# Hybrid decoder layer: token rows, row factors and transposes in the first stage, 128-wide diagonal products and row ends

## The chip, the cores and the metric

The kernel runs on one core of one Trainium2 chip (trn2). The metric is device microseconds of one execution. Three timed runs of the kernel before took 1751.09, 1756.36 and 1757.32 us (median 1756.36). A separate profiled execution, from which all rows below are taken, took 1752.65 us.

## The reference

The layer has 2048 tokens and a model width of 1024, in float32. A condition vector `c` gives a shift, a scale and a gate per feature. The normalised tokens are modulated, projected to 4096 columns, used by two kinds of attention, gated and projected back:

```python
mod = (c @ w_ada + b_ada).astype(jnp.float32)
shift, scale, gate = jnp.split(mod, 3, axis=-1)
h = (_rmsnorm(x, norm_g) * (1.0 + scale[:, None, :]) + shift[:, None, :])
proj = h @ w_in       # sb_q, sb_k, sb_v, sb_g (512 each), df_q, df_k, df_v, df_g (512 each)
sb_out = _stick_breaking(...) * silu(sb_g)      # 8 heads of 64, strictly causal
df_out = _rmsnorm(_diff_attention(...), subln_g) * 0.8 * silu(df_g)   # 4 heads, two 64-wide maps each
out = concatenate([sb_out, df_out]) @ w_out
x = x + gate * out
```

`_rmsnorm` divides each token's row by the root of the mean of its squares over the 1024 features. The stick-breaking weight is `sigmoid(z_ts) * prod(1 - sigmoid(z_tj))` over the keys between s and t; the differential head is the difference of two softmaxes.

## The kernel before, in words

Every product of float32 matrices is split into a high and a low half (`hH`/`hL` of the activations, `wh`/`wl` of the weights, in the float32r type), and is the sum of three products (`mm3`, L318 to L320). The program is written as one long list of steps; a scheduler then sets the order on each engine by the dependences and its own estimate of times. Work with a later due time (`P`, the projections) is woven between the steps of the attention (`A`) by a planner with fixed costs (L1055 to L1166).

The first stage is what happens before the attention can start. It works on the first 1024 tokens in two chunks of 512:

- The chunk's `x` is loaded turned, feature rows by tokens, as eight tiles `xt` of 128x512 from `xT` (L68, L239). ScalarE squares them (L206, L209), VectorE adds the squares up (`xacc`, L210), TensorE turns the sums (`ps_c`, L198), and VectorE reduces them (L199) to a sum per token and makes the factor `rs_y` by eleven small instructions after L216 (L132 to L141: three steps of Newton's method). TensorE spreads the factor over the partitions (`ps_y`, L223), ScalarE copies it to `rb` (L226), and VectorE or GpSimd multiplies the eight tiles with it (L915, L918; L977 in the second chunk).
- Beside it the shift and the scale are made: `ada_block` (L163, L165) takes a 128x1024 tile `wada` of `w_ada`, multiplies it with `c` spread over the partitions (`cb`, loaded by a DMA at L899 into one of the six large buffers of tag `big`) and sums each row. There are two tiles for each 128 features (k), 16 in all, of 512 KB each; `gmul` (L947) is (1 + scale) times the norm's gain.
- `make_h` (L245 to L251) then makes `hH` and `hL` of one k: ScalarE's Identity with scale and bias, a cast, and a subtraction on VectorE or GpSimd.
- For each k, TensorE adds twelve 512-wide products to four PSUM tiles (`ps_p` for q, `ps_k` for k); these are followed by the v products of the chunk (`ps_n`, four blocks of 24 products, 256 wide), and by the same for the second chunk (q at 512 wide, then k, then v).
- Weights arrive as `raw` or `kraw` tiles (L299) and are split by a cast and a subtraction (L302/L304 and L306).
- Twenty transposes of the identity (L907) stand on TensorE ahead of the first sums.

All loads are issued by SyncE's queue, in order; each waits for its destination to be free and for an earlier DMA of its slot.

In the attention, a query block of 128 rows takes its scores against the keys in segments of 512 (`scores`, L482; the mask of the diagonal is one more 128-wide product, L485). Where the last segment is 128 keys long, it is computed 256 wide (`segs`). The weights of a pair of query blocks are turned (`ps_t`, L518), split into `aH` and `aL` (L524, L525) and multiplied with v (`av`, L598/L599 and L671 to L673), 256 queries wide. In the last group of keys of a pair the first 128 columns are zeros, written by two memsets on GpSimd (L522, L523).

Of the kernel before, what the change touches and what calls it, by code (L numbers as in the profile page):

```python
# [45 lines left out]
def build(ctx: ExitStack, tc, xT, cT, normg, w_adaT, b_ada, w_in, qg, kg, lam4, subg, w_out,  # L46
# [42 lines left out]
    def more_constants():  # L89
        nc.sync.dma_start(qgt, qg)  # L90
        nc.sync.dma_start(kgt, kg)
        nc.sync.dma_start(sgt, subg)
        tmp0 = ppool.tile([128, 512], F32, name="tmp0", tag="stg", bufs=NSTG)
        lamt = tmp0[:, 0:256].rearrange("p (f d) -> p f d", d=64)
        nc.sync.dma_start(lamt, lam4.unsqueeze(0).broadcast_to([128, 4, 64]))
        for h in range(NDF):
# [14 lines left out]
        nc.sync.dma_start(dist, distd)  # L111
# [131 lines left out]
    def make_h(k, ch, xt, hH, hL, act, pool=False):  # L243
        th, tl = hH[(k, ch)], hL[(k, ch)] = h_tiles(k, ch)
        nc.scalar.activation(xt, xt, AF.Identity, scale=gmul[:, k:k + 1], bias=mod[:, k:k + 1])  # L245
        if act:
            nc.scalar.copy(th, xt)
        else:
            nc.gpsimd.tensor_scalar(out=th, in0=xt, scalar1=1.0, scalar2=0.0, op0=ALU.mult,
                                    op1=ALU.add)  # L250
        (nc.gpsimd if pool else nc.vector).tensor_tensor(out=tl, in0=xt, in1=th.bitcast(F32),  # L251
                                                         op=ALU.subtract)
# [236 lines left out]
    def segs(n, ext):  # L489
        return [(o, min(512, n - o), min(512, ext - o, max(256, n - o))) for o in range(0, n, 512)]  # L490
# [10 lines left out]
    def back_steps(pair, A, get_av, acol, vmm):  # L501
# [3 lines left out]
        def up(st, g):  # L505
# [15 lines left out]
            if last:  # L521
# [376 lines left out]
    cb = big("cb")[:, 0:D]  # L898
    nc.sync.dma_start(cb, cT.unsqueeze(0).broadcast_to([128, D]))  # L899
    acc = stage("xacc")  # L900
    for k in range(KT):
        sq_add(acc, k, xa[0][k], nc.vector)

    def warm(n):
        wp = aps_.tile([128, 512], F32, name="av", tag="av")
        for j in range(n):
            nc.tensor.transpose(wp[:, 0:128], ident, ident)  # L907

    y0 = row_rstd(acc, nc.vector)
    warm(WARM[0])  # L910
    rb = spread(y0)
    warm(WARM[1])
    rs0 = rs_last[0]
    for k in range(3):
        nc.vector.tensor_tensor(out=xa[0][k], in0=xa[0][k], in1=rb, op=ALU.mult)  # L915
    w_q = load_w(w_in, C_SBQ, False)
    for k in range(3, KT):
        nc.gpsimd.tensor_tensor(out=xa[0][k], in0=xa[0][k], in1=rb, op=ALU.mult)  # L918
    w_k, kwl = [], None
    wa = {}  # L920
    for j in range(KT):
# [12 lines left out]
    def load_v():
        for kk in range(4):
            vwh = apool.tile([128, 2, 256], F32R, name="vwh", tag="kc", bufs=8)
            vwl = apool.tile([128, 2, 256], F32R, name="vwl", tag="kc", bufs=8)
            w_v.extend(load_w_part(w_in, C_SBV, kk, vwh, vwl))

    def load_x1():  # L940
        for k in range(KT):
            xa[1][k] = load_x(0, 1, k, apool.tile([128, 512], F32, name="xt", tag="vc", bufs=8))
    pq = [pps.tile([128, 512], F32, name="ps_p", tag="pj") for _ in range(2)]
    pk = [zps.tile([128, 512], F32, name="ps_k", tag="z") for _ in range(2)]
    for k in range(KT):
# [3 lines left out]
        ada_block(0, k, wa[(0, k)], cb)  # L949
        make_h(k, 0, xa[0][k], *hs[0], True, k in (2, 4, 6))  # L950
# [7 lines left out]
    after(ld, load_x1)  # L958
    acc = stage("xacc")
    for k in range(KT):  # L960
        sq_add(acc, k, xa[1][k], nc.vector)
# [207 lines left out]
_INS = ["xT", "cT", "normg", "w_adaT", "b_ada", "w_in", "qg", "kg", "lam4", "subg", "w_out",  # L1169
# [45 lines left out]
```

## Time and profile before

| | |
|---|---|
| timed runs (median of 3) | 1756.36 us |
| profiled execution | 1752.65 us |
| its span in the trace | 1750.9 us |
| TensorE busy | 1657.7 us (95%), 10740 matmuls |
| VectorE, ScalarE, GpSimd busy | 1258.4, 990.3, 890.0 us (72%, 57%, 51%) |
| first product of q and k starts | 42.44 us |
| first chunk's q and k done | about 72.6 us |
| second chunk's first product starts | 93.10 us |
| second chunk's q done, its k starts | 105.31 us |

Busy time of TensorE is counted from start to modelled end of each matmul, and consecutive matmuls overlap; what one costs in a dense stream is the distance between two starts. The granted clock is 1.00 where TensorE runs at 2.4 GHz, and 0.50 at 1.2 GHz.

### The profile page before, as it was taken

To read this page: it belongs to the slowest core of one execution; us is meant where nothing else is said; L and a number is where in the kernel's file an instruction comes from. 1 tells how busy PE (TensorE), PEld (TensorE's weight loads), DVE (VectorE), ACT (ScalarE), POOL (GpSimd) and SP (SyncE) were. 2 spreads that over 40 slices of the span, in tenths; PEclk is the share of its full clock that TensorE was granted. 3 is DMA by queue.
4 is the path that set the end of the run, shared out by engine and by line. 5 is a ranking of instruction groups with operands and counts; after the bars stand their busy time and mean duration, and the time that the engine had idled before them with its cause. 6 is when DMAs were issued, how large, how long until landed. Compare 5 with 4: busy or idle time off the path is not lost.

```text
span 1750.9 us, 31674 instructions
## 1 busy us (share of the span) xinstructions
PE 1657.7 (95%) x10740; PEld 1486.7 (85%) x10740; DVE 1258.4 (72%) x2558; ACT 990.3 (57%) x1997; POOL 890.0 (51%) x1454
## 2 busy tenths in 40 slices
PE   1889989999999999999999999999999999999999
PEld 1677879789999989878898888799998988888887
DVE  6735645776657786767787877878888888888741
ACT  2335555555645444656776777777765645555521
POOL 5425464556635663565655655667433353323553
PEclk7999999999999999999999999999999999999999
DMA  7757767653564876434433333234433566434264
GB/s 254 228 151 211 217 187 226 190 163 85 164 181 135 254 240 187 157 106 121 121 101 105 97 109 97 79 94 131 133 88 116 162 204 203 130 127 134 86 216 149
DMA packets 212689, 268.65 MB, mean 153 GB/s; under 512 B 21296, under 2 KB 136240, under 8 KB 212400
## 3 DMA queue, kind: packets, MB, share of 16 engines
q1 hardware_dynamic: 212528, 266.64, 50.5%
q8 instruction: 85, 1.39, 0.3%
q14 instruction: 76, 0.62, 0.1%
HBM read 186.86 MB, written 79.69 MB: 152 GB/s over the span
## 4 chain that ended last, share of the span: by engine, by line
PE 69%; DVE 6%; DMA 4%; POOL 3%; issue 3%; ACT 2%; SPq 0%; DVEq 0%; ACTq 0%; POOLq 0%
PE ps_z L482 11%; PE ps_t L518 8%; PE ps_n L318 6%; PE ps_n L320 6%; PE ps_n L319 6%; PE ps_p L318 4%; PE ps_p L320 4%; PE ps_p L319 4%; PE av L599 3%; PE av L598 3%; PE ps_o L319 3%; PE ps_o L318 3%; PE ps_o L320 3%; PE av L672 1%; DMA xt<-in_xT 1%
## 5 line engine op out<-in xcount | busy, mean ns | idle before, releaser
L621 POOL TENSOR_TENSOR s<-s,u 128x512 f32<-128x512 f32 (+4 forms) x320 | 307.2, 962 | 213.1 <-DVE u L617 190.0
L482 PE MATMUL ps_z<-kc,qc 128*128 128x512 f32 (+2 forms) x1280 | 360.3, 376 | 9.4 <-DVE u L617 6.9
L524 ACT CAST aH<-ps_t 128x512 fp32r<-128x512 f32 (+1 forms) x432 | 240.7, 567 | 169.3 <-PE ps_t L518 159.5
L525 DVE TENSOR_TENSOR aL<-ps_t,aH 128x512 fp32r<-128x512 f32 (+1 forms) x432 | 276.3, 650 | 76.3 <-ACT aH L524 74.3
L318 PE MATMUL ps_n<-wh,hH 128*128 128x256 f32 x960 | 274.4, 286 | 2.4 <-DVE sl L327 1.2
L306 POOL TENSOR_TENSOR wl<-raw,wh 128x512 fp32r<-128x512 f32 x168 | 225.8, 1352 | 93.2 <-ACT wh L302 85.4
L319 PE MATMUL ps_n<-wl,hH 128*128 128x256 f32 x960 | 271.6, 284 | 1.0 <-POOL wl L306 1.0
L320 PE MATMUL ps_n<-wh,hL 128*128 128x256 f32 x960 | 272.3, 284 | 0.0
L617 DVE TENSOR_TENSOR_SCAN u<-ps_z,u,dist 128x512 f32<-128x512 f32 x192 | 245.6, 1279 | 33.8 <-ACT ps_z L614 27.7
L482 PEld LDWEIGHTS ps_z<-kc,qc 128*128 128x128 f32 x1280 | 210.9, 189 | 36.5 <-DVE u L617 11.9
L713 ACT ACTIVATE e<-e,nm 128x1024 f32<-128x1024 f32 (+4 forms) x192 | 171.9, 898 | 116.4 <-DVE nm L711 109.0
L699 DVE CUSTOM_DVE_ANT_0 e<-ps_z,dist 128x512 f32<-128x512 f32 (+3 forms) x320 | 186.9, 603 | 52.0 <-PE ps_z L482 44.5
L613 ACT ACTIVATE s<-ps_z 128x512 f32<-128x512 f32 (+3 forms) x320 | 172.9, 540 | 75.6 <-PE ps_z L482 38.9
L318 PE MATMUL ps_p<-hH,wh 128*128 128x512 f32 x480 | 192.5, 405 | 12.0 <-issue 11.2
L319 PE MATMUL ps_p<-hL,wh 128*128 128x512 f32 x480 | 189.7, 395 | 3.7 <-DVE hL L251 2.3
L320 PE MATMUL ps_p<-hH,wl 128*128 128x512 f32 x480 | 189.2, 395 | 0.0
L318 PEld LDWEIGHTS ps_n<-wh,hH 128*128 128x128 f32 x960 | 183.0, 191 | 6.9 <-issue 1.6
L319 PEld LDWEIGHTS ps_n<-wl,hH 128*128 128x128 f32 x960 | 183.2, 191 | 4.5 <-POOL wl L306 1.2
L320 PEld LDWEIGHTS ps_n<-wh,hL 128*128 128x128 f32 x960 | 183.3, 191 | 1.7
L614 ACT ACTIVATE ps_z<-ps_z 128x512 f32<-128x512 f32 (+3 forms) x320 | 173.2, 541 | 0.0
L518 PE MATMUL ps_t<-ident,s 128*128 128x128 f32 x1088 | 167.6, 274 | 5.2 <-DVE aL L525 4.9
L598 PE MATMUL av<-aH,vc 128*128 128x256 f32 x576 | 162.5, 294 | 7.4 <-ACT aH L524 6.3
(171 smaller groups left out, 3500.3 us busy)
## 6 DMA issues: line engine op xcount, KB each, us to landing
qc<-qst SPq DMA_DIRECT2D x256, 128.0 KB, 3.2
raw<-in_w_in SPq DMA_DIRECT2D x124, 256.0 KB, 3.3
kc<-kst SPq DMA_DIRECT2D x96, 256.0 KB, 3.5
xt<-in_xT SPq DMA_DIRECT2D x48, 256.0 KB, 4.7
vc<-vst SPq DMA_DIRECT2D x48, 256.0 KB, 3.1
vc<-vdt SPq DMA_DIRECT2D x48, 256.0 KB, 3.6
raw<-in_w_out SPq DMA_DIRECT2D x48, 256.0 KB, 3.4
wada<-in_w_adaT SPq DMA_DIRECT2D x16, 512.0 KB, 5.8
```

The costliest lines, as they stand in the source:

```text
L306: nc.gpsimd.tensor_tensor(out=wl, in0=raw, in1=wh.bitcast(F32), op=ALU.subtract)
L318: nc.tensor.matmul(ps, lhsT=aH, rhs=bH, start=first, stop=False)
L319: nc.tensor.matmul(ps, lhsT=aH, rhs=bL, start=False, stop=False)
L320: nc.tensor.matmul(ps, lhsT=aL, rhs=bH, start=False, stop=last)
L482: last_pe[0] = nc.tensor.matmul(ps[:, :w], lhsT=q[:, pt, tl], rhs=kch[k0 // 512][:, :w], start=pt == 0, stop=pt == 1 and diag is None)
L518: nc.tensor.transpose(tp[:, pos * 256 + t * 128:pos * 256 + t * 128 + 128], A[t][0][:, sb * 128:sb * 128 + 128], ident)
L524: nc.scalar.copy(aH[:, f0:], tp[:, f0:])
L525: nc.vector.tensor_tensor(out=aL[:, f0:], in0=tp[:, f0:], in1=aH[:, f0:].bitcast(F32), op=ALU.subtract)
L598: nc.tensor.matmul(o, lhsT=v, rhs=aH, start=st, stop=False)
L617: nc.vector.tensor_tensor_scan(out=u[:, c0:c0 + w][:, ::-1], data0=ur, data1=dist[:, :w], initial=1.0 if top else u[:, c0 + w:c0 + w + 1], ...
L621: nc.gpsimd.tensor_tensor(out=s[:, c0:c0 + m], in0=s[:, c0:c0 + m], in1=u[:, c0 + 1:c0 + m + 1], op=ALU.mult)
L699: nc.vector.tensor_tensor_reduce(out=e[m][:, c0 + o:c0 + o + w], in0=ps[:, :w], in1=dist[:, d0:d0 + w], scale=1.0, scalar=-3e38, op0=ALU.a ...
```

## The change

There are two parts.

**The first stage.** The tokens' rows are loaded as they are (`xn`, 128 tokens by 512 features, eight tiles per chunk, from a new input `xN`, which is the same `x` unturned). In the first chunk ScalarE's squares write their row sums at once (`accum_out`); in the second ScalarE does four and VectorE four. `row_factors` makes the factor of a token in 12 instructions. It is a column now, one value per partition, and the eight tiles are multiplied with it in place, four on VectorE and four on ScalarE. TensorE turns them (`turn`: four 128x128 transposes for each k), and `make_h` works from the PSUM tile. The column sums, the spread, `xacc` and `rb` of this stage are gone.

`c` is no longer spread by a DMA, but by eight transposes of a 128x8 tile into two PSUM tiles (`ps_cb`), so `ada_block` is two 512-wide halves; the bias enters as the first half's starting value. The casts of the q, k and v weights are on ScalarE (they were on GpSimd), and half of v's subtractions on VectorE. The weights of q and k are loaded between the `wada` tiles, two for every two k; v's raw weights go into one large buffer. Six of the eight `hL` subtractions of the first chunk are on GpSimd (three before). The 20 transposes of the identity are 40 plain products. `dist` (1 MB) is loaded after k's results are stored, and the lambda constants after the second chunk's factors.

**Diagonal products and row ends.** A last segment of 128 keys is computed 128 wide. In the last group of keys of a pair, the product with the second key block takes only the 128 columns that are not zero, unless it is the only group; so the two memsets are left out there.

```diff
-    xa = [[None] * KT, [None] * KT]
-    for k in range(KT):
-        xa[0][k] = apool.tile([128, 512], F32, name="xt", tag="kc", bufs=8)
-        nc.sync.dma_start(xa[0][k], xT[k * 128:(k + 1) * 128, 0:512])
+    def load_xn(ch, tag):
...
+                xt = apool.tile([128, 512], F32, name="xn", tag=tag, bufs=8)
+                t0 = ch * 512 + t * 128
+                x_last[0] = nc.sync.dma_start(xt, xN[t0:t0 + 128, f * 512:f * 512 + 512])
...
     def ada_block(third, j, wt, cb):
         m = third * 8 + j
-        nc.vector.tensor_tensor_reduce(out=wt, in0=wt, in1=cb, scale=1.0, scalar=0.0, op0=ALU.mult,
-                                       op1=ALU.add, accum_out=mod[:, m:m + 1])
-        nc.vector.tensor_tensor(out=mod[:, m:m + 1], in0=mod[:, m:m + 1], in1=badat[:, m:m + 1],
-                                op=ALU.add)
+        part = col.tile([128, 1], F32, name="part", tag="adas", bufs=1)
+        for i, (ini, acc) in enumerate(((badat[:, m:m + 1], part), (part, mod[:, m:m + 1]))):
+            ws = wt[:, i * 512:i * 512 + 512]
+            nc.vector.tensor_tensor_reduce(out=ws, in0=ws, in1=cb[i], scale=1.0, scalar=ini,
+                                           op0=ALU.mult, op1=ALU.add, accum_out=acc)
...
+    def row_squares(xn, nv=4):
...
+                if t < nv:
+                    nc.scalar.activation(junk[(f * 4 + t) % 2 if nv == 4 else 0], xn[f][t], AF.Square, accum_out=acc)
+                else:
+                    nc.vector.tensor_tensor_reduce(out=junk[1], in0=xn[f][t], in1=xn[f][t],
...
+    def scale_rows(xt, y, t, eng):
+        if eng is nc.scalar:
+            nc.scalar.activation(xt, xt, AF.Copy, scale=y[:, t:t + 1])
+        else:
+            eng.tensor_scalar(out=xt, in0=xt, scalar1=y[:, t:t + 1], scalar2=None, op0=ALU.mult)
+
+    def turn(ps, xn, k):
+        for t in range(4):
+            nc.tensor.transpose(ps[:, t * 128:(t + 1) * 128],
+                                xn[k // 4][t][:, (k % 4) * 128:(k % 4) * 128 + 128], ident)
+
+    def make_h(k, ch, ps, hH, hL, pool):
...
+        xt = stage("xh") if pool else ps
+        nc.scalar.activation(xt, ps, AF.Identity, scale=gmul[:, k:k + 1], bias=mod[:, k:k + 1])
+        nc.scalar.copy(th, xt)
...
     def segs(n, ext):
-        return [(o, min(512, n - o), min(512, ext - o, max(256, n - o))) for o in range(0, n, 512)]
+        return [(o, min(512, n - o), min(512, n - o)) for o in range(0, n, 512)]
...
-            if last:
+            if last and ng == 1:
                 nc.gpsimd.memset(aH[:, 0:128].bitcast(F32), 0.0)
                 nc.gpsimd.memset(aL[:, 0:128].bitcast(F32), 0.0)
...
-                vmm(av[:, acol:acol + 256], sb, aH[:, o:o + 256], aL[:, o:o + 256],
+
+                n0 = 128 if ng > 1 and gi == 0 and bi == 1 else 0
+                vmm(av[:, acol + n0:acol + 256], sb, aH[:, o + n0:o + 256], aL[:, o + n0:o + 256],
                     gi == 0 and bi == 0, gi == ng - 1 and bi == 1)
...
+    cb = [tps.tile([128, 512], F32, name="ps_cb", tag="tr") for _ in range(2)]
+    for j in range(KT):
+        nc.tensor.transpose(cb[j // 4][:, (j % 4) * 128:(j % 4) * 128 + 128],
+                            ckt[:, j:j + 1].broadcast_to([128, 128]), ident)
...
+    ss0 = row_squares(xn0)
+    y0 = row_factors(ss0)
+    pk = [zps.tile([128, 512], F32, name="ps_k", tag="z") for _ in range(2)]
+    xps = [zps.tile([128, 512], F32, name="ps_x", tag="z"),
+           aps_.tile([128, 512], F32, name="av", tag="av")]
+
+    for j in range(WARM):
+        nc.tensor.matmul(xps[1][:, 0:128], lhsT=identr, rhs=identr, start=True, stop=True)
+    for f in range(2):
+        for t in range(4):
+            scale_rows(xn0[f][t], y0, t, nc.vector if t < 2 else nc.scalar)
...
+    turn(xps[0], xn0, 0)
     for k in range(KT):
...
+        make_h(k, 0, xps[k % 2], *hs[0], k in POOL_H)
+        if k + 1 < KT:
+            turn(xps[(k + 1) % 2], xn0, k + 1)
```

**What moves on the engines.** VectorE, at the start of the program. `wada` is the tile of `w_ada`, `mod` its row sums, `ps_c` and `xss` the sums of squares, `rs_i` and `rs_y` the factor. Before:

```order
L210 TENSOR_TENSOR xacc<-xacc,xsq 128x512 x7
L163 ISA wada,mod<-wada,cb 128x1024
L163 ISA mod 128x1
L199 TENSOR_REDUCE xss<-ps_c 128x4
L165 TENSOR_TENSOR mod<-mod,badat 128x1
L216 TENSOR_SCALAR xv<-xss 128x4
L132 TENSOR_SCALAR rs_i<-xv 128x4
L134 TENSOR_SCALAR rs_y<-rs_i 128x4
```

Now, from the program's first VectorE instruction (its three Newton steps are L288 to L291; one of them is shown):

```order
L276 SCALAR_TENSOR_TENSOR xv<-xss_292 128x4
L281 TENSOR_SCALAR rs_i<-xv 128x4
L283 TENSOR_SCALAR rs_y<-rs_i 128x4
L288 TENSOR_TENSOR rs_t<-rs_y 128x4
L289 SCALAR_TENSOR_TENSOR rs_t<-rs_t,xv 128x4
L291 SCALAR_TENSOR_TENSOR rs_y<-rs_t,rs_y 128x4
...
L179 ISA wada,part<-wada,ps_cb,badat 128x512
L179 ISA part 128x1
L300 TENSOR_SCALAR xn<-xn,rs_y 128x512 x4
L179 ISA wada,mod<-wada,ps_cb,part 128x512
L179 ISA mod 128x1
L1015 SCALAR_TENSOR_TENSOR gmul<-mod,ngt 128x1
```

The factor no longer stands behind seven additions and a product with a `wada` tile; its first input is now ScalarE's row sums.

ScalarE, at the same place. Before, after the squares it has nothing until the spread factor (`rb`) and the first `gmul`:

```order
L206 ACTIVATE xacc<-xt 128x512
L209 ACTIVATE xsq<-xt 128x512 x7
L73 CAST ident<-idraw 128x128
L226 COPY rb<-ps_y 128x512
L245 ACTIVATE xt<-xt,mod,gmul 128x512
L247 CAST hH_0_377<-xt 128x512
L245 ACTIVATE xt<-xt,mod,gmul 128x512
L247 CAST hH_0_399<-xt 128x512
```

Now:

```order
L267 ACTIVATE xsq,xss_292<-xn 128x512 x8
L298 ACTIVATE xn<-xn,rs_y 128x512 x4
L365 CAST wh<-raw 128x512
L365 CAST kwh<-kraw 128x512
L310 ACTIVATE ps_x<-ps_x,mod,gmul 128x512
L311 CAST hH_0_384<-ps_x 128x512
L310 ACTIVATE xh<-av,mod,gmul 128x512
L311 CAST hH_0_412<-xh 128x512
```

Four multiplications and two casts of weights have come between the squares and the first `hH`.

TensorE, at the end of the first chunk's v products and the start of the second chunk's q (`hH_1` and `hL_1` are the second chunk's halves). Before:

```order
L318 MATMUL ps_n<-vwh,hH_0_531 128x256
L319 MATMUL ps_n<-vwl,hH_0_531 128x256
L320 MATMUL ps_n<-vwh,hL_0_532 128x256
L318 MATMUL ps_p<-hH_1_814,wh 128x512
L319 MATMUL ps_p<-hL_1_815,wh 128x512
L320 MATMUL ps_p<-hH_1_814,wl 128x512
```

Now:

```order
L383 MATMUL ps_n<-vwh,hL_0_587 128x256
L381 MATMUL ps_p<-hH_1_799,wh 128x512
L304 MATMUL ps_x<-ident,xn 128x128 x4
L382 MATMUL ps_p<-hL_1_800,wh 128x512
L383 MATMUL ps_p<-hH_1_799,wl 128x512
L381 MATMUL ps_p<-hH_1_809,wh 128x512
```

The transposes of the second chunk stand between its products, a group of four ahead of each k's.

## Rows read from the trace of the kernel before

**Rows 1.** Windows by stage: busy us (and instructions) per engine, TensorE's clock, DMA share, GB/s

```profile
0.00:42.40 42.40, 5.90 (x28) 4.86 (x28) 29.12 (x42) 8.53 (x13) 25.15 (x29) 0.71 0.75 262
42.40:72.60 30.20, 26.24 (x96) 19.17 (x96) 28.24 (x54) 15.23 (x25) 17.52 (x16) 0.90 0.68 226
72.60:93.10 20.50, 15.57 (x104) 14.88 (x105) 12.50 (x35) 5.58 (x12) 3.22 (x6) 0.83 0.68 175
...
150.00:1750.90 1600.90, 1557.67 (x10231) 1402.98 (x10228) 1171.58 (x2404) 939.73 (x1906) 825.65 (x1386) 1.00 0.49 147
```

**Rows 2.** Timeline of the first 43 us: start us, us, what, [idle before <-releaser]

```profile
5.88 4.67 ACT L209 ACTIVATE xsq<-xt 128x512 f32<-128x512 f32 x7 [1.39 <-DMA xt<-in_xT]
...
17.64 1.48 DVE L163 CUSTOM_DVE_ANT_0 wada<-wada,cb 128x1024 f32<-128x1024 f32 x1 [5.62 <-DMA wada<-in_w_adaT]
...
29.93 0.16 DVE L141 TENSOR_TENSOR rs_y<-rs_y,rs_t 128x4 f32<-128x4 f32 x1
...
40.70 0.14 DVE L947 SCALAR_TENSOR_TENSOR gmul<-mod,ngt 128x1 f32<-128x1 f32 x1
...
42.44 1.19 PE L318 MATMUL ps_p<-hH,wh 128*128 128x512 f32 x2 [11.18 <-issue]
```

**Rows 3.** Timeline of the second chunk's factor and of TensorE behind it

```profile
76.97 0.17 DVE L216 TENSOR_SCALAR xv<-xss 128x4 f32<-128x4 f32 x1
...
79.77 0.16 DVE L141 TENSOR_TENSOR rs_y<-rs_y,rs_t 128x4 f32<-128x4 f32 x1
...
86.15 0.29 DVE L101 TENSOR_TENSOR tmp<-tmp 128x128 f32<-128x128 f32 x1 [5.15 <-DMA tmp<-in_lam]
...
87.81 0.58 PE L318 MATMUL ps_n<-vwh,hH 128*128 128x256 f32 x1 [3.92 <-DVE stv L405]
```

**Rows 4.** Groups by line and form: operation xcount | busy us, mean ns | idle before

```profile
L699 DVE CUSTOM_DVE_ANT_0 e<-ps_z,dist 128x512 f32<-128x512 f32 x224 | 149.6, 684 | 42.1 <-PE ps_z L482 35.0 <-PE ps_t L518 5.8
L713 ACT ACTIVATION_READ_ACCUMULATOR e<-e,nm 128x1 f32 x192 | 36.0, 187 | 0.0
L245 ACT ACTIVATE xt<-xt,mod,gmul 128x512 f32<-128x512 f32 x16 | 12.5, 812 | 21.6 <-DVE gmul L947 19.8 <-DVE mod L165 1.0 <-DVE xt L977 0.8
L306 POOL TENSOR_TENSOR kwl<-kraw,kwh 128x512 fp32r<-128x512 f32 x4 | 5.0, 1258 | 0.0
L306 POOL TENSOR_TENSOR vwl<-raw,vwh 128x512 fp32r<-128x512 f32 x4 | 7.3, 1823 | 0.3
L977 DVE TENSOR_TENSOR xt<-xt,rb 128x512 f32<-128x512 f32 x8 | 5.3, 734 | 0.0
L522 POOL MEMSET aH<- 128x128 f32 x96 | 19.6, 205 | 95.2 <-PE av L598 64.0 <-PE av L673 16.3 <-DVE aL L525 6.6
```

**Rows 5.** TensorE's starts in dense streams, between 381 and 392 us

```profile
381.27 0.39 PE L318 MATMUL ps_p<-hH,wh 128*128 128x512 f32 x1
...
382.63 0.51 PE L482 MATMUL ps_z<-kc,qc 128*128 128x384 f32 x2
...
387.36 0.63 PE L482 MATMUL ps_z<-kc,qc 128*128 128x512 f32 x2
387.82 0.22 PE L485 MATMUL ps_z<-maskr,ident 128*128 128x128 f32 x1
...
388.05 0.28 PE L319 MATMUL ps_n<-wl,hH 128*128 128x256 f32 x1
...
389.01 0.28 PE L318 MATMUL ps_n<-wh,hH 128*128 128x256 f32 x1
...
390.81 0.49 PE L518 MATMUL ps_t<-ident,s 128*128 128x128 f32 x3
...
391.26 0.28 PE L319 MATMUL ps_n<-wl,hH 128*128 128x256 f32 x1
```

**Rows 6.** Windows: clock and DMA rate inside the first chunk's products

```profile
42.40:48.70 6.30, 5.60 (x12) 3.97 (x13) 6.30 (x16) 2.47 (x4) 0.00 (x0) 0.50 0.67 218
48.70:60.00 11.30, 10.42 (x46) 8.26 (x45) 11.30 (x25) 4.27 (x7) 5.30 (x4) 1.00 1.04 353
```

More of the change, by code (lines that the diff above doesn't have):

```diff
@@ L73, in build @@
     nc.scalar.copy(identr, idraw)
+    ckt = col.tile([128, KT], F32, name="ckt", tag="qss", bufs=2)
+    nc.sync.dma_start(ckt, cK)
+    xn0 = load_xn(0, "kc")
     badat = ctile([128, 24], "badat")
@@ L240, in load_x @@
         return xt
-    def make_h(k, ch, xt, hH, hL, act, pool=False):
-        th, tl = hH[(k, ch)], hL[(k, ch)] = h_tiles(k, ch)
[L245 to L250, printed above, removed]
+    def row_squares(xn, nv=4):
+        ss = col.tile([128, 8], F32, name="xss8", tag="xss", bufs=1)
+        junk = [stage("xsq") for _ in range(2)] if nv == 4 else None
+        if junk is None:
+            wide = big("xsq")
+            junk = [wide[:, 0:512], wide[:, 512:1024]]
+        for f in range(2):
+            for t in range(4):
+                acc = ss[:, f * 4 + t:f * 4 + t + 1]
+                if t < nv:
+                    nc.scalar.activation(junk[(f * 4 + t) % 2 if nv == 4 else 0], xn[f][t], AF.Square, accum_out=acc)
+                else:
+                    nc.vector.tensor_tensor_reduce(out=junk[1], in0=xn[f][t], in1=xn[f][t],
+                                                   scale=1.0, scalar=0.0, op0=ALU.mult, op1=ALU.add,
+                                                   accum_out=acc)
+        return ss
@@ new lines, in row_factors @@
+    def row_factors(ss):
+        v = col.tile([128, 4], F32, name="xv", tag="xv", bufs=1)
+        nc.vector.scalar_tensor_tensor(out=v, in0=ss[:, 0:4], scalar=D * EPS, in1=ss[:, 4:8],
+                                       op0=ALU.add, op1=ALU.add)
+        ti = col.tile([128, 4], I32, name="rs_i", tag="rs_i", bufs=1)
+        y = col.tile([128, 4], F32, name="rs_y", tag="rs_y")
+        t = col.tile([128, 4], F32, name="rs_t", tag="rs_t", bufs=2)
+        nc.vector.tensor_scalar(out=ti, in0=v.bitcast(I32), scalar1=1, scalar2=None,
+                                op0=ALU.logical_shift_right)
+        nc.vector.tensor_scalar(out=y.bitcast(I32), in0=ti, scalar1=-1, scalar2=0x5F3759DF,
+                                op0=ALU.mult, op1=ALU.add)
+        for i in range(3):
+            g = 32.0 if i == 2 else 1.0
+            nc.vector.tensor_tensor(out=t, in0=y, in1=y, op=ALU.mult)
+            nc.vector.scalar_tensor_tensor(out=t, in0=t, scalar=-0.5 * g, in1=v, op0=ALU.mult,
+                                           op1=ALU.mult)
+            last = nc.vector.scalar_tensor_tensor(out=y, in0=t, scalar=1.5 * g, in1=y, op0=ALU.add,
+                                                  op1=ALU.mult)
+        rs_last[0] = last
+        return y
@@ L895, in build @@
     ev_q, ev_k = ev_qk(qst, C_SBQ), ev_qk(kst, C_SBK)
[L898 to L919, printed above, removed]
+    cb = [tps.tile([128, 512], F32, name="ps_cb", tag="tr") for _ in range(2)]
+    for j in range(KT):
+        nc.tensor.transpose(cb[j // 4][:, (j % 4) * 128:(j % 4) * 128 + 128],
+                            ckt[:, j:j + 1].broadcast_to([128, 128]), ident)
+    w_q, w_k, kwl = [], [], None
     wa = {}
@@ L957, in build @@
     after(ld, load_v)
[L958 to L961, printed above, removed]
+    xn1 = after(w_last[0], lambda: load_xn(1, "vc"))
+    xl = x_last[0]
+    ss1 = row_squares(xn1, 2)
     for s in range(2):
@@ L965, in build @@
         ev_k(pk[s], C_SBK + s * 128, 0, 0)
+    kst_last = st_last[0]
     v_steps = proj_N(get_h0, 0, C_SBV, ev_v, {"w": w_v}, True)
-    after(ld, more_constants)
+    after(kst_last, lambda: nc.sync.dma_start(dist, distd))
     for c, f in v_steps[:2]:
         f()
-    y1 = row_rstd(acc, nc.vector)
+    y1 = row_factors(ss1)
+    for f in range(2):
+        for t in range(4):
+            scale_rows(xn1[f][t], y1, t, nc.vector if t < 2 else nc.scalar)
     for c, f in v_steps[2:6]:
         f()
-    rb = spread(y1)
-    for c, f in v_steps[6:8]:
-        f()
     for k in range(KT):
-        nc.vector.tensor_tensor(out=xa[1][k], in0=xa[1][k], in1=rb, op=ALU.mult)
-        make_h(k, 1, xa[1][k], *hs[0], k % 2 == 0)
+        if k in (2, 4):
+            v_steps[5 + k // 2][1]()
+        xp = tps.tile([128, 512], F32, name="ps_x", tag="tr")
+        turn(xp, xn1, k)
+        make_h(k, 1, xp, *hs[0], False)
+    after(rs_last[0], more_constants)
     P = []
```

53 lines of the change are left out of this document (35 added, 18 removed).

## The prediction

> **What bounds the kernel now.** I read the windows by stage first. After 150 us TensorE is busy 1557.67 of 1600.90 us [rows 1]: there it sets the pace, and only 43 us of its idle time are left. Before that it is not: in the first 42.4 us it is busy 5.90 us, and in the stage from 72.6 to 93.1 us 15.57 of 20.5 at a mean clock of 0.83. So a first stage that feeds TensorE earlier moves all that follows to the left, and an edit to later products is worth what it takes off TensorE's starts.
>
> Then the timeline of the start, to see which wait ends last. The squares end at 10.55 us (5.88 + 4.67), but the factor is ready at 30.09 [rows 2]: VectorE stands 5.62 us behind a product with a `wada` tile whose load comes late, and its small instructions run beside GpSimd's weight splits. Then follow the spread, three of the scalings on VectorE and the first `gmul` at 40.70; the first product starts at 42.44. How slow those small instructions were shows in the second chunk, where GpSimd has nothing to do: 15 of them take 2.96 us there (76.97 to 79.93), 0.2 us each [rows 3]. The second chunk has its own stall: VectorE sits behind the lambda constants' load until 86.15, and TensorE waits 3.92 us for an evacuation queued behind it [rows 3].
>
> **The change part by part.** Durations come from one execution of 1752.65 us (span 1750.9 and 1.75 around it); it lies 3.7 below the median of the timed runs and inside their spread, and the sum is made against it.
>
> *Up to the first product: 42.44 us now, about 21 then.* ScalarE's squares carry a row sum each (0.187 us, rows 4), and two small loads stand ahead of `x`; I put their end at 12.0 us in place of 10.55. The additions, the turning and the reduction go, and nothing stands ahead of the factor on VectorE: 12 instructions of 0.2 us, 14.4 us. GpSimd has only tiny instructions then. Next on VectorE, by the order: a half tile, four scalings, a half tile, `gmul`, two half tiles. A half tile with one input in PSUM has a row of its own kind, 0.684 us [rows 4], 0.7 with its sum read out: 2.8. A scaling with a column has no row; its bounds are 0.16 (the same engine on 128x4, rows 3) and 0.73 (two tiles of this size, rows 4); I take 0.5, nearer to the row of its size: 2.0. That makes 19.3 us. ScalarE's four scalings (0.6 to 0.8 each, rows 4) and two weight casts end at about 17.9, under VectorE's cover. From `gmul` to the first product it took 1.74 us (40.70 to 42.44); then 21.0. What must have landed by then is 4 MB at most, against 262 GB/s in the first 42 us [rows 1]: 15 us.
>
> *The first chunk's q and k: done at 72.6 now, about 48 then.* 512-wide products start 0.227 us apart (six in 381.27 to 382.63), transposes 0.11 apart ((391.26 - 390.81 - 0.12)/3, with 0.12 for a 256-wide product, eight in 388.05 to 389.01) [rows 5]. The clock was 0.50 for 6.3 us after the first product [rows 6]; the 40 products put ahead end some 7 us before the first real one, so I count the first twelve at twice the distance, 5.5 us (2.7 if the clock is full). Then 84 x 0.227 = 19.1 and six groups of four transposes 2.6. Together 27.2: 48.2 us. The covers: VectorE needs four half tiles and a `gmul` per k, 2.9 us, under TensorE's 3.2 (12 x 0.227 + 4 x 0.11). GpSimd needs two weight subtractions and two of `hL` for two k, at 1.26 us each 5.0 under 6.3; at 1.82, the row of v's weights [rows 4], it is 7.3, and adds 3 to 4 us over the chunk. Zero to 4; I take zero, since VectorE's sums there no longer read two tiles from SBUF, as they did beside the 1.82.
>
> [...]
>
> *The loads.* 12.6 MB must land for the last k (2.1 of `x`, 8.4 of `wada`, 2.1 of weights). At the 353 GB/s of 48.7 to 60 us [rows 6] that is 36 us after some 2 of start; with 2.9 for its half tiles, 1.7 to `hH` and 2.7 of products, 45 us, so they stay hidden by 3 us. In the order five `wada` pairs are issued before the first waits for a buffer, since `cb` no longer holds one.
>
> *v of the first chunk: 20.5 us now, 13.4 then.* 96 x 0.12 = 11.5 and eight transposes 0.9. The lambda load no longer stands ahead of an evacuation. What is late next is the second chunk's factor: on both engines it stands behind the evacuation of the second v block (48.2 + 5.8), so the scaled rows come at about 58, the first `hH` at 61.3, and TensorE is through at 60.6: a wait of about 1 us. q of the second chunk then starts at 61.6 in place of 93.1. There 48 x 0.227 = 10.9 and 24 transposes 2.6, with ScalarE about as busy (8 x 1.4 and four casts); 1.5 of waits: 15.0 in place of 12.2, and k starts at 76.6 in place of 105.3. That is -28.7 us (-22 to -34 with the bounds). From there the two programs do the same work.
>
> *The narrow products.* In a head's 16 query blocks four have a last segment of 128 keys: 8 x 4 x 2 + 4 x 2 x 4 x 2 = 128 score products. Seven of eight pairs have a narrow row end: 8 x 7 x 2 + 4 x 7 x 3 = 196. A 128-wide product of this type is in the trace already, the mask: between 387.36 and 388.05 stand two of 512, the mask and one of 256, so the mask takes 0.69 - 0.45 - 0.12 = 0.12, a transpose 0.11 [rows 5], and a 256-wide product 0.12. The gain is 0 to 0.01 us each, 0 to 3.2 us in all; I take 3.
>
> *The memsets.* 168 of 0.205 us go from GpSimd, which waited 80 us for `av` to free their tiles [rows 4]. But TensorE waits for GpSimd hardly anywhere in the 43 us; -3 to +1, and I take 0.
>
> The sum: 1752.65 - 28.7 - 3 = 1721 us. The likeliest case's own range is 1712 to 1731.
>
> **The rivals.** *The loads set the pace.* In the first two stages they ran at 262 and 226 GB/s [rows 1]. At 262 the 12.6 MB take 48 us and the first chunk ends at 55 instead of 48: 1728. Against it: those means hold times in which the queue waited for buffers.
>
> *Narrow products cost half.* If the distance went with the width, 0.06 instead of 0.12, 324 of them would give 19 us instead of 3: 1705. Against it are the mask's 0.12 and the transposes' 0.11, where the next weights must be loaded as well. The Trainium skill (TensorE: Matmul & The Clock Gate, Back-to-back issue gap) has 134 cycles for 128 columns and 262 for 256, which would give 17 us by an estimate from that page; the rows here do not agree.
>
> *Narrow products cost more, and the result is slower.* The kernel before pads these segments to 256, as one would if a float32r product under that width lost its rate. At a quarter of the rate each takes as long as 512 columns, 0.227: 324 x 0.107 = +35 us, 1724 + 35 = 1759. It decides the sign from 0.21 us per product (0.12 + 29/324). The mask's 0.12 speaks against it.
>
> *The later order costs TensorE.* The scheduler has woven some projection blocks elsewhere, and scores, scans and subtractions meet other neighbours. If the 43 us of idle time after 150 us grow by a third: +14, 1735.
>
> **How the numbers follow.** Forecast 0.70, loads 0.13, half-cost products 0.06, later order 0.08, slower 0.03. A measurement of this kernel can tell about 0.5%, 9 us, from no change. The first four all lie below 1743, save a tail of the fourth and of sums of two: faster 0.94, same 0.04, slower 0.02. The range 1708 to 1738 holds the forecast, the loads and the later order, and leaves out the half-cost products and the slow case.
>
> **What would show it.** In the new profile: the factor at 14 to 15 us; the first 512-wide product at 20 to 23; the last of the first chunk's k at 46 to 52; the second chunk's k from 74 to 82. Narrow score products 0.11 to 0.12 us from their neighbours. TensorE idle after the first stage about as now. It would be wrong if the first product came after 30 us (then a load or VectorE holds the factor), if TensorE's groups in the first chunk were 4 us or more apart (GpSimd or the loads), or if the idle time after 150 us were over 55 us.

## The result, and the profile after

The changed kernel takes 1735.02 us (median of four, 1733.63 to 1737.08), the kernel before 1755.57 beside it: ratio 0.9885, 95% interval 0.9866 to 0.9903. The whole interval lies below 1, so it is faster, by some 20 us where 32 were forecast, and the time is inside the forecast's range (1708 to 1738). The profiled execution took 1733.63 us, its span 1731.8: 19 us less than that of before.

| us from the span's start | before | forecast | after |
|---|---|---|---|
| first 512-wide product | 42.44 | 21.0 | 20.11 |
| first chunk's q and k through, v starts | 72.6 | 48.2 | 55.65 |
| second chunk's first product | 93.10 | 61.6 | 69.25 |
| second chunk's k starts | 105.31 | 76.6 | 86.56 |
| end of the span | 1750.9 | 1719.3 | 1731.8 |

The windows by stage, columns as in [rows 1]:

```profile
0.00:20.10 20.10, 12.34 (x56) 11.67 (x56) 6.56 (x26) 11.98 (x26) 4.46 (x13) 1.00 0.89 302
20.10:25.00 4.90, 4.89 (x12) 3.88 (x13) 4.72 (x13) 0.99 (x2) 0.00 (x0) 1.00 1.04 407
25.00:55.00 30.00, 26.26 (x110) 17.48 (x108) 27.58 (x58) 16.30 (x30) 19.01 (x15) 1.00 0.83 295
55.00:68.90 13.90, 12.67 (x105) 12.43 (x104) 9.05 (x29) 7.79 (x17) 1.04 (x3) 1.00 0.84 198
68.90:86.20 17.30, 14.73 (x72) 10.99 (x72) 6.86 (x14) 11.43 (x21) 3.88 (x3) 1.00 0.46 147
...
131.00:1731.80 1600.80, 1556.28 (x10234) 1400.79 (x10232) 1171.49 (x2404) 938.83 (x1906) 796.31 (x1221) 1.00 0.49 147
```

In the third line VectorE is busy 27.58 of 30 us: it sets the first chunk's pace, as e1 and e2 below show, and not TensorE. TensorE's 26.26 counts modelled ends; its 84 products and 24 transposes of that stretch need 84 x 0.227 + 24 x 0.11 = 21.7 us at the distances of [rows 5]. The end of the run is as it was: 44.5 us idle in 1600.8, against 43.2 in [rows 1].

The timeline of the start (start us, us, what, idle before and releaser). It answers to [rows 2]:

```profile
11.59 0.16 DVE L276 SCALAR_TENSOR_TENSOR xv<-xss 128x4 f32<-128x4 f32 x1 [11.59 <-ACT xsq L267]
...
13.77 0.16 DVE L291 SCALAR_TENSOR_TENSOR rs_y<-rs_t,rs_y 128x4 f32<-128x4 f32 x1
...
14.61 1.67 DVE L300 TENSOR_SCALAR xn<-xn,rs_y 128x512 f32<-128x512 f32 x4
...
16.98 0.16 DVE L1015 SCALAR_TENSOR_TENSOR gmul<-mod,ngt 128x1 f32<-128x1 f32 x1
...
20.11 1.22 PE L381 MATMUL ps_p<-hH,wh 128*128 128x512 f32 x2 [2.99 <-ACT hH L311]
```

The factor is ready at 13.93 us and the four scalings take 1.67. Now VectorE inside the first chunk's loop over k, two periods of it:

```profile
25.50 1.29 DVE L1015 SCALAR_TENSOR_TENSOR gmul<-mod,ngt 128x1 f32<-128x1 f32 x1
26.72 0.73 DVE L179 CUSTOM_DVE_ANT_0 wada<-wada,ps_cb,badat 128x512 f32<-128x512 f32 x1
...
29.08 0.75 DVE L179 CUSTOM_DVE_ANT_0 wada<-wada,ps_cb,part 128x512 f32<-128x512 f32 x1
29.75 0.08 DVE L179 DVE_READ_ACCUMULATOR2_ANT mod<- 128x1 f32 x1
29.87 1.29 DVE L1015 SCALAR_TENSOR_TENSOR gmul<-mod,ngt 128x1 f32<-128x1 f32 x1
...
34.23 1.29 DVE L1015 SCALAR_TENSOR_TENSOR gmul<-mod,ngt 128x1 f32<-128x1 f32 x1
```

and GpSimd at the same times:

```profile
25.48 1.29 POOL L312 TENSOR_TENSOR hL<-xh,hH 128x512 fp32r<-128x512 f32 x1 [5.88 <-ACT hH L311]
...
29.86 1.28 POOL L312 TENSOR_TENSOR hL<-xh,hH 128x512 fp32r<-128x512 f32 x1 [0.58 <-ACT hH L311]
...
34.21 1.29 POOL L312 TENSOR_TENSOR hL<-xh,hH 128x512 fp32r<-128x512 f32 x1 [3.07 <-ACT hH L311]
```

`gmul` works on one column, and takes 0.16 us where it does not start beside a GpSimd subtraction of `hL` (16.98, 22.27). From the third k on it starts 0.01 to 0.02 us behind a GpSimd subtraction, and takes as long as that, 1.29. The loop's period is 4.36 us (25.50, 29.87, 34.23): four half tiles of 0.79 with their sums, 3.15, and 1.21 for `gmul`.

In the second chunk the lambda constants stand in VectorE's way again, 3.38 us in place of the 5.15 in [rows 3], now between two subtractions of `hL`:

```profile
70.16 0.68 DVE L312 TENSOR_TENSOR hL<-ps_x,hH 128x512 fp32r<-128x512 f32 x1
74.22 0.29 DVE L115 TENSOR_TENSOR tmp<-tmp 128x128 f32<-128x128 f32 x1 [3.38 <-issue]
74.55 0.29 DVE L116 TENSOR_REDUCE ldot<-tmp 128x2 f32<-128x128 f32 x1
74.75 0.68 DVE L312 TENSOR_TENSOR hL<-ps_x,hH 128x512 fp32r<-128x512 f32 x1
```

The load was issued at 67.80, behind the stores of v. "issue" means that the profile shows no releaser; the tile that L115 reads is the load's.

### The profile page after: what moved, and what is told of

Same layout as the page of the kernel before. It is cut to its first block, busy times and chain, and to the rows that moved or that the text cites. A ratio compares the mean times of both kernels' runs of the same rounds, so it can differ in the third digit from the quotient of the medians.

```text
span 1731.8 us, 31619 instructions
## 1 busy us (share of the span) xinstructions
PE 1669.4 (96%) x10816; PEld 1494.2 (86%) x10816; DVE 1236.3 (71%) x2556; ACT 1000.3 (58%) x2027; POOL 836.6 (48%) x1266
## 4 chain that ended last, share of the span: by engine, by line
PE 64%; DVE 8%; DMA 4%; issue 4%; POOL 3%; ACT 3%; SPq 1%; DVEq 0%; ACTq 0%; POOLq 0%
PE ps_z L547 10%; PE ps_t L583 8%; PE ps_n L381 5%; PE ps_n L383 5%; PE ps_n L382 5%; PE ps_p L381 4%; PE ps_p L383 4%; PE ps_p L382 4%; PE av L666 3%; PE av L665 3%; PE ps_o L381 3%; PE ps_o L382 3%; PE ps_o L383 3%; DMA xt<-in_xT 2%; DVE u L684 1%
## 5 line engine op out<-in xcount | busy, mean ns | idle before, releaser
L547 PE MATMUL ps_z<-kc,qc 128*128 128x512 f32 (+3 forms) x1280 | 358.8, 374 | 10.5 <-DVE u L684 7.9
L547 PEld LDWEIGHTS ps_z<-kc,qc 128*128 128x128 f32 x1280 | 210.8, 190 | 37.4 <-DVE u L684 13.4
```

Of the source, the lines that this page charges most:

```text
L547: last_pe[0] = nc.tensor.matmul(ps[:, :w], lhsT=q[:, pt, tl], rhs=kch[k0 // 512][:, :w], start=pt == 0, stop=pt == 1 and diag is None)
```

## The experiments

**gmul on ScalarE (e1).** The theory: `gmul`, with its two tensor inputs in SBUF, stands behind GpSimd's whole subtraction, and VectorE's row of work sets the period. The rival: the loads, or the passing of `hH` and `hL` between the engines, set it.

```diff
-        nc.vector.scalar_tensor_tensor(out=gmul[:, k:k + 1], in0=mod[:, 8 + k:9 + k], scalar=1.0,
-                                       in1=ngt[:, k:k + 1], op0=ALU.add, op1=ALU.mult)
+        nc.scalar.activation(gmul[:, k:k + 1], mod[:, 8 + k:9 + k], AF.Identity,
+                             scale=ngt[:, k:k + 1], bias=ngt[:, k:k + 1])
```

> The changed kernel with one edit: gmul is made by ScalarE (Identity of the scale, with the gain as factor and as bias) instead of VectorE; TensorE's, GpSimd's and SyncE's instructions stay as they are. In the changed kernel the first chunk's k loop has a period of 4.36 us, and in it gmul takes 1.28 us on VectorE each time it starts together with a GpSimd subtraction. Theory (VectorE's small instruction with two SBUF inputs stands behind GpSimd's subtraction, and VectorE's row of work sets the period): the period falls to VectorE's four half tiles, 4 x 0.79 = 3.2 us; over six to seven k that is 6 to 7.5 us, the first chunk's last product starts at 47.5 to 49 instead of 54.65, and the run takes 1727 to 1730 us, if nothing behind the chunk eats it. Rival (the loads, or the passing of hH and hL between ScalarE, GpSimd and TensorE, set the 4.36 us, and gmul only fills a wait): the period stays above 4.2 us and the time at 1735 within 1 us.

1730.21 us (ratio 0.9840, 0.9812 to 0.9868), the upper end of the theory's range. TensorE's groups of a k in this run, and the window of the chunk:

```profile
36.32 0.71 PE L381 MATMUL ps_p<-hH,wh 128*128 128x512 f32 x2
...
39.53 0.71 PE L381 MATMUL ps_p<-hH,wh 128*128 128x512 f32 x2
...
49.30 0.38 PE L381 MATMUL ps_n<-vwh,hH 128*128 128x256 f32 x1 [0.99 <-DVE sl L392]
```

```profile
20.00:48.00 28.00, 27.60 (x120) 22.04 (x120) 25.06 (x61) 19.91 (x38) 19.77 (x15) 1.00 1.06 385
```

The period is 3.21 us, TensorE is busy 27.60 of 28, and v starts at 49.30 in place of 55.65. The loads ran at 385 GB/s, and neither TensorE nor VectorE waited for one, so the loads' rival falls, and with it the prediction's, though the 55 us that it gave for the end of the chunk (55.65 measured) had come true. Of the 6.35 us, 6.31 are left at the second chunk's k (80.25), and some 5 between the medians (1735.02 and 1730.21), each measured beside its own runs of the kernel before; by the ratios to those it is 8.

**gmul as one tensor and a column (e2).** Does the wait hang on the form of the instruction? The edit leaves it at its place and changes only the form.

```diff
-        nc.vector.scalar_tensor_tensor(out=gmul[:, k:k + 1], in0=mod[:, 8 + k:9 + k], scalar=1.0,
-                                       in1=ngt[:, k:k + 1], op0=ALU.add, op1=ALU.mult)
+        nc.vector.tensor_scalar(out=gmul[:, k:k + 1], in0=mod[:, 8 + k:9 + k], scalar1=1.0,
+                                scalar2=ngt[:, k:k + 1], op0=ALU.add, op1=ALU.mult)
```

> The changed kernel with gmul still on VectorE and at the same place, but with one tensor input (the scale) and the gain as a column operand, where it was an instruction with two tensor inputs. Nothing else moves on any engine. Theory A (two tensor inputs from SBUF are what holds it behind GpSimd): gmul falls from 1.28 to about 0.16 us and the period from 4.36 to 3.3 us; 1728 to 1731 us. Theory B (any small VectorE instruction from SBUF to SBUF is held, or one with the column operand is too): gmul stays at about 1.28 us and the time at 1735 within 1 us.

1729.95 us (0.9851, 0.9822 to 0.9880), as e1. VectorE, then GpSimd, at the same moment:

```profile
25.77 0.21 DVE L1015 TENSOR_SCALAR gmul<-mod,ngt 128x1 f32<-128x1 f32 x1
25.90 0.74 DVE L179 CUSTOM_DVE_ANT_0 wada<-wada,ps_cb,badat 128x512 f32<-128x512 f32 x1
...
29.06 0.21 DVE L1015 TENSOR_SCALAR gmul<-mod,ngt 128x1 f32<-128x1 f32 x1
```

```profile
25.75 1.29 POOL L312 TENSOR_TENSOR hL<-xh,hH 128x512 fp32r<-128x512 f32 x1 [5.98 <-ACT hH L311]
```

It starts 0.02 us behind the same subtraction and takes 0.21 us in place of 1.29; the period is 3.29. So theory A holds for `gmul`: without the second tensor input it does not wait, at the same size and place. That a VectorE instruction with one tensor input never waits does not follow. In the kernel before, one of the factor's small instructions has one tensor and two constants (L139, 128x4), and it waits as well:

```profile
23.19 1.26 POOL L306 TENSOR_TENSOR kwl<-kraw,kwh 128x512 fp32r<-128x512 f32 x1
23.27 1.21 DVE L139 TENSOR_SCALAR rs_t<-rs_t 128x4 f32<-128x4 f32 x1
...
29.73 0.17 DVE L139 TENSOR_SCALAR rs_t<-rs_t 128x4 f32<-128x4 f32 x1
```

It takes 1.21 us beside a GpSimd subtraction of 1.26, and 0.17 without one. What sets it apart from e2's `gmul` (four elements for one, constants for a column) was not tested.

**The two parts apart (e3, e4).** e3 is the changed kernel with 256-wide segments, row ends and the memsets; e4 the kernel before with the narrow ones alone.

```diff
-        return [(o, min(512, n - o), min(512, n - o)) for o in range(0, n, 512)]
+        return [(o, min(512, n - o), min(512, ext - o, max(256, n - o))) for o in range(0, n, 512)]
...
-            if last and ng == 1:
+            if last:
...
-                n0 = 128 if ng > 1 and gi == 0 and bi == 1 else 0
+                n0 = 0
```

(e4 makes the same edits the other way round in the kernel before.)

> The changed kernel with its second part undone: last segments 256 wide, row ends 256 wide, and the two memsets back; the first stage as in the changed kernel. Theory (the narrow products are worth 0 to 1 us, because 324 of them cost 0.11 to 0.12 us either way): 1735 to 1736 us, ratio to the kernel before 0.988 to 0.989. The prediction's value (3 us): 1738, ratio 0.990. Rival (narrow products cost half, 19 us): 1754, ratio 0.999.

> The kernel before with the second part alone: last segments and row ends 128 wide, memsets left out where the products are narrow; the first stage as before. Theory: 0 to 1 us less than before, 1754.5 to 1755.5, ratio 0.999 to 1.000. The prediction's value: 1752.5, ratio 0.998. Rival (half cost): 1737, ratio 0.989.

e3: 1737.26 us, ratio 0.9889 (0.9867 to 0.9911); the changed kernel, run again (e8, below), 0.9885. e4: 1755.27, ratio 0.9980 (0.9962 to 0.9998). By the ratios the narrow products are worth 0.7 us by the one pair (some 6 either way, by the two intervals) and 3.5 by the other (3 either way; by the medians 1.4, 1756.70 to 1755.27): both agree with the theory's 0.4 to 1 and with the prediction's 3, and neither with 19. The window of e3 after the first stage shows no more of it:

```profile
131.00:1733.60 1602.60, 1561.69 (x10249) 1405.44 (x10247) 1171.49 (x2408) 939.96 (x1908) 828.19 (x1389) 1.00 0.49 147
```

TensorE is busy 5.4 us longer than in the changed kernel's window above, but idle for 40.9 in place of 44.5; a second execution of the changed kernel (e8) was busy 1562.33. GpSimd is rid of 31.9 us (828.19 to 796.31), mostly the memsets, and the time does not show it.

**Row products split in two (e6).** The price of one narrow product is too small to be seen in the time, so it was multiplied.

```diff
-            nc.tensor.matmul(o, lhsT=v, rhs=aH, start=st, stop=False)
-            last_pe[0] = nc.tensor.matmul(o, lhsT=v, rhs=aL, start=False, stop=sp)
+            for c in ([0] if st else range(0, aH.shape[-1], 128)):
+                cs = slice(c, aH.shape[-1] if st else c + 128)
+                nc.tensor.matmul(o[:, cs], lhsT=v, rhs=aH[:, cs], start=st, stop=False)
+                last_pe[0] = nc.tensor.matmul(o[:, cs], lhsT=v, rhs=aL[:, cs], start=False,
+                                             stop=sp and cs.stop == aH.shape[-1])
```

> The changed kernel with every 256-wide product of the stick-breaking heads' row sums that does not open a group made as two 128-wide ones: 912 products of 256 columns become 1824 of 128, with the same result. This multiplies what a 128-wide product costs. Theory (a 128-wide product costs 0.11 to 0.12 us in the stream, as the mask and the transposes do, against 0.12 for 256 columns): 912 x (2 x 0.113 - 0.119) = +98 us, 1833 us, and 1820 to 1845 with these bounds. Rival (half cost, 0.06 us): no change, 1735 us. Rival (a quarter of the rate, 0.21 us): 912 x (0.42 - 0.119) = +275 us, 2010.

1812.84 us (two runs; ratio 1.0322, 1.0281 to 1.0362), 76.5 above the changed kernel on the same chip (e8). 76.5 / 912 = 0.084 for each product added, so a 128-wide one costs (0.084 + 0.119) / 2 = 0.10 us by the time: below the 1820 of the theory's range, far from both rivals. Part of the added work went into TensorE's idle time, as the windows after the first stage show. Here:

```profile
131.00:1808.80 1677.80, 1644.55 (x11151) 1497.78 (x11149) 1173.18 (x2404) 940.62 (x1906) 799.16 (x1221) 0.99 0.47 140
```

In e8:

```profile
131.00:1734.20 1603.20, 1562.33 (x10235) 1406.73 (x10233) 1170.38 (x2404) 939.19 (x1906) 800.68 (x1221) 0.99 0.49 147
```

It is idle for 33.3 us in the one (1677.80 - 1644.55) and 40.9 in the other. With these 7.6 us a narrow product costs (84.1 / 912 + 0.119) / 2 = 0.106 us. The stream shows one more reason why the mean lies under 0.11:

```profile
1008.90 0.28 PE L667 MATMUL av<-aH,vc 128*128 128x256 f32 x1
1009.02 0.28 PE L668 MATMUL av<-aL,vc 128*128 128x256 f32 x1
1009.14 0.22 PE L667 MATMUL av<-aH,vc 128*128 128x128 f32 x1
1009.20 0.28 PE L668 MATMUL av<-aL,vc 128*128 128x128 f32 x1
1009.31 0.28 PE L667 MATMUL av<-aH,vc 128*128 128x128 f32 x1
```

The first narrow product behind a wide one is followed after 0.06 us, the next ones after 0.11. In the changed kernel, where narrow products come in pairs, the wide one behind them gives most of that back: starts at 366.93 and 366.99 (narrow), 367.10 and 367.27 (wide), so these three take 0.34 where three wide ones take 0.36. At 0.102 the 324 narrow products would be worth (0.119 - 0.102) x 324 = 5.5 us of TensorE's stream, at 0.106 4.2, at 0.01 each 3.2; the timed pairs lie at 0.7 and 3.5. e6 multiplied row products only; the price of the 128 narrow score products rests on e3 and e4.

**Lambda constants earlier (e5).** On e1: the load stands behind the second chunk's token rows, and its product and sum with it.

```diff
+    def lambda_sums():
+        tmp0 = ppool.tile([128, 512], F32, name="tmp0", tag="stg", bufs=NSTG)
+        lamt = tmp0[:, 0:256].rearrange("p (f d) -> p f d", d=64)
+        nc.sync.dma_start(lamt, lam4.unsqueeze(0).broadcast_to([128, 4, 64]))
...
     def more_constants():
...
-        lamt = tmp0[:, 0:256].rearrange("p (f d) -> p f d", d=64)
-        nc.sync.dma_start(lamt, lam4.unsqueeze(0).broadcast_to([128, 4, 64]))
...
     xl = x_last[0]
+    after(xl, lambda_sums)
```

> The kernel with gmul on ScalarE (e1) and one more edit: the lambda constants' load stands behind the second chunk's token rows, ahead of the stores of q, k and v, so that VectorE's product and sum of them come before the second chunk's factor. In e1 they came at 67.89 us, after VectorE had stood 3.39 us and ScalarE 2.85 us, and TensorE 1.42 us behind hL; k of the second chunk started at 80.25. Theory (the wait for that load holds the second chunk): VectorE's stall is gone, k of the second chunk starts 1 to 3 us earlier, at 77.3 to 79.2, and the run takes 1727 to 1729 us where e1 took 1730. Rival (ScalarE's two passes and its weight casts set the pace there anyway, or the added work delays the second factor as much): k starts at 80 to 81 us and the time is e1's.

1729.74 us (0.9854, 0.9825 to 0.9883). The sums now stand at 52.28 without a wait, and TensorE in the second chunk:

```profile
63.39 0.73 PE L384 MATMUL ps_p<-hH,wh 128*128 128x512 f32 x2 [1.47 <-ACT hH L314]
...
78.72 0.50 PE L384 MATMUL ps_p<-hH,kwh 128*128 128x512 f32 x1 [0.99 <-DVE sl L395]
```

The second chunk's k starts 1.53 us earlier than in e1 (78.72 for 80.25), as the theory had it, though the stage begins 0.49 later (63.39 for 62.90): the scalings start 0.17 later behind the factor, and ScalarE now copies a block of v (0.38) ahead of the first `hH`. The stage itself takes 15.3 us in place of e1's 17.3, where the prediction had 15.0. In the run's time 1.5 us cannot be told from none.

**Shared squares as well (e7), and the changed kernel again (e8).**

```diff
...
-    ss0 = row_squares(xn0)
+    ss0 = row_squares(xn0, 2)
...
```

(The rest of the edit keeps the squares' scratch tiles in both chunks as they were.)

> The kernel of e5 (gmul on ScalarE, lambda constants earlier) with the first chunk's squares shared: ScalarE squares four of the eight tiles and VectorE four, as in the second chunk. In e1 ScalarE's eight squares ended at 11.85 us and VectorE had nothing to do before 11.88. Theory (the squares on one engine hold the factor): they end with the last tile's landing, about 10 us, the factor comes at 12.2 to 12.8 instead of 14.2, the first 512-wide product at 18.5 to 19.2 instead of 20.36, and the run takes 1 to 2 us less than e5: 1725 to 1728. Rival (the first wada tile or the first weights set the first product): the factor comes earlier, the first product stays at 20 to 20.4 us, and the time is e5's.

> The changed kernel itself, on the same chip as e5 to e7. Theory: 1734 to 1737 us, ratio to the kernel before 0.987 to 0.990; the second chunk's k from 86 to 87 us. It gives the size of the gains of e5 and e7 without a change of chip; there is no rival to it.

e7: 1725.48 us (0.9836, 0.9809 to 0.9862); e8: 1736.30 (0.9885, 0.9860 to 0.9911), its second chunk's k at 86.77. e7's time lies in the expected range, but the mechanism expected of its edit was wrong:

```profile
10.11 0.69 DVE L272 CUSTOM_DVE_ANT_0 xsq<-xn 128x512 f32<-128x512 f32 x1 [2.21 <-DMA xn<-in_xN]
...
10.84 0.69 DVE L272 CUSTOM_DVE_ANT_0 xsq<-xn 128x512 f32<-128x512 f32 x1
```

VectorE waits for the last tile but one until 10.11 us and then squares the last two, one after the other, to 11.54, as late as ScalarE alone was through with all eight (11.56 in the changed kernel). ScalarE's share ends at 10.16. So the factor comes at 13.99 and the first product at 20.12: the late loads hold it, and the two squares that stand in a row behind them. Whether these two, one on each engine, would be done sooner was not run. What e7 has over e8 is what e1 and e5 gave, 8.3 us at the second chunk's k (86.77 to 78.49). It has the lowest median here, 10.8 us below the changed kernel's; the 4 us between e5 and e7 have no place in the first stage's trace, and the two intervals overlap, so e7 is not shown to be faster than e5.

## Why the prediction was right in its sign and 13 us off in its size

**Up to the first product: right.** Forecast 21.0, measured 20.11. The factor came at 13.93 (14.4 said); a scaling took 0.4 us (0.5 taken, bounds 0.16 and 0.73). (Behind L216 the factor took 14 small instructions in the kernel before, not the eleven of its description; the prediction's 15 with L216 are right.)

**The first chunk's q and k: the step that failed.** Forecast 27.2 us, measured 35.5 (20.11 to 55.65). The failing sentence is "VectorE needs four half tiles and a `gmul` per k, 2.9 us, under TensorE's 3.2": it took 4.36. Two terms were mis-sized. The four half tiles take 3.15, not 2.8, because a half tile is 0.75 us long, not 0.684 [rows 4], and its sum is read behind it; with a `gmul` that waits for nobody this makes 3.29 (e2), 0.1 over TensorE's 3.2. And `gmul` was left some 0.1 us, where 1.21 was needed. It has 0.14 in [rows 2], and 0.14 to 0.15 in seven of its eight places in the kernel before; in the eighth it has 0.58, beside a GpSimd cast of 0.61. The prediction asked how far VectorE slows GpSimd, and put GpSimd's subtractions at 1.26 us if the sums read PSUM; that was right (1.28 to 1.30). It did not ask what GpSimd does to the one small instruction with two tensor inputs. e1 and e2 show it: without that wait the period is 3.21 to 3.29, and v starts at 49.30 and 49.96. e1's chunk takes 28.9 us (20.36 to 49.30); in what is left over the 27.2 TensorE waits 0.99 us for an evacuation (finished sums that VectorE takes out of PSUM) at v's start (0.61 in the changed kernel), a wait that the prediction put at nothing.

The price could be read in the kernel before. There other one-column instructions with two tensor inputs, the additions of the bias (L165), stand around `gmul`, and the waits fell on them:

```profile
49.17 1.31 POOL L251 TENSOR_TENSOR hL<-xt,hH 128x512 fp32r<-128x512 f32 x1 [8.41 <-ACT hH L247]
...
49.27 1.24 DVE L165 TENSOR_TENSOR mod<-mod,badat 128x1 f32<-128x1 f32 x1
...
51.57 0.15 DVE L165 TENSOR_TENSOR mod<-mod,badat 128x1 f32<-128x1 f32 x1
51.64 0.15 DVE L947 SCALAR_TENSOR_TENSOR gmul<-mod,ngt 128x1 f32<-128x1 f32 x1
```

The change takes L165 away (the bias is a starting value now) and puts twice as many `hL` subtractions on GpSimd, so that from the third k on `gmul` meets one each time. The prediction saw that small instructions run slowly beside GpSimd's splits, for the factor, and did not carry it over to `gmul`.

The Trainium skill has a rule for this (SBUF — State Buffer, Who interferes with whom): a VectorE instruction with two SBUF inputs contends with a GpSimd instruction that reads SBUF. By the Trainium skill too (SBUF — State Buffer, Summary: rules for kernel authors), the second of the two to issue blocks until the first is through. The trace agrees to the number: 1.29 us behind a subtraction of 1.29, 0.21 with one tensor input. The prediction argued in this way for the large instructions alone ("VectorE's sums there no longer read two tiles from SBUF").

The clock term was right: the first twelve products stood 0.43 to 0.5 us apart and ended near 25.2 (5.5 us said, 5.1 measured).

**The loads: right that they stay hidden.** Even with the period at 3.21 (e1) TensorE never waited for one in the chunk.

**v of the first chunk: right.** 13.6 us from v's start to the second chunk's first product (13.4 said), with the forecast wait for `hH`, 0.97.

**The second chunk's q: 17.3 us, 15.0 said.** The prediction took the lambda load out of the path of the first chunk's v and did not look where it went. It came back here: 3.38 us of VectorE and 1.43 of TensorE; without it the stage takes 15.3 (e5).

Together: -0.9, +8.3, +0.2 and +2.3 make the 10 us by which the second chunk's k came late (86.56 for 76.6). With both mended (e5) it starts at 78.72. The bounds of that gain had been "-22 to -34"; the measured 18.75 lies outside them, since `gmul` beside GpSimd had no bound of its own. With the narrow products' 3 us, of which these two executions show 0.35, the 10 us become the 12.6 between 1721 and the profiled 1733.63. That 1735 still lies inside the range is luck: the room up there was left for the loads and the later order, and neither took place.

**The narrow products: 3 us forecast, not resolved.** From the second chunk's k to the end both programs take 1645 us (1645.59 and 1645.24). The price per row product was about right (0.10 to 0.106 measured, 0.11 to 0.12 said), the rivals of half cost and of a quarter of the rate are refuted (e6), and the pairs of e3 and e4 hardly tell 3 us from none: e4's interval starts at 0.4.

**The memsets at nothing: not shown apart,** since e3 and e4 move them together with the narrow products. The idle time after the first stage was right (44.5 us from 131 us on, under the 55 at which the text called itself wrong). Of its signs, the last of the first chunk's k (54.65, 46 to 52 said) and the second chunk's k (86.56, 74 to 82 said) failed. And "groups in the first chunk were 4 us or more apart (GpSimd or the loads)", one of those by which it called itself wrong, came true: the engine was GpSimd, by way of VectorE.

## What to carry to other kernels

When work moves between VectorE and GpSimd, list every VectorE instruction that runs on SBUF tiles, the smallest ones too: each can cost a whole GpSimd instruction. Those with two tensor inputs come first; a column operand in place of the second tensor freed the one here. One tensor input alone is no guarantee (L139), so look for a small instruction of the same form in a trace where GpSimd works beside it. Work of 2.9 us under 3.2 is hardly covered: add its gaps and its reads of sums before you call it hidden. A load or a constant that is taken out of one stage's path is to be followed to the place where it lands next.

## What the runs showed of the hardware

- A 128x1 instruction on VectorE with two tensor inputs took 1.29 us in place of 0.16, ending with the GpSimd subtraction that had started 0.02 us earlier; with a column operand 0.21 us (e2); on ScalarE 0.39 (e1).
- A 128x4 instruction on VectorE with one tensor input and two constants took 1.21 us beside a GpSimd subtraction of 1.26, and 0.17 without one (the kernel before, 23.27 and 29.73).
- Narrow products in a row start 0.11 us apart. The first one behind a wide one is followed after 0.06, and where wide and narrow ones are mixed a narrow one costs 0.10 to 0.106 on average (e6).
- From 21.12 to 24.96 us the 512-wide products stood 0.43 us apart, nearly twice the 0.227 of later, while the granted clock's column reads 1.00 there; in the kernel before the same distance went with 0.50 [rows 6]. By the distances TensorE ran at the lower level (1.2 GHz) there; why the column does not show it stays open. Before it came forty plain products (to 13.34 us), an idle 1.8 us, eight transposes and an idle 3.0 us.
